# A rotary key of 32 rows: from a three-product step of its own to plain float32 products between the gates

## The chip, the cores and the metric

The kernel runs on one core of a Trainium2 chip. The metric is the device time of one execution in microseconds (us). An execution of the kernel before takes 1001.8 us, the median of 3 runs (998.82 to 1003.82).

The engines are named as the profile names them: PE is TensorE (PEld its weight loads), DVE is VectorE, ACT is ScalarE, POOL is GpSimd, SP is the engine that issues nearly all DMAs here (SPq its queue). Each engine takes its instructions in the order in which they were written, so an instruction that waits holds back all that stand behind it on that engine.

## The reference, cut to what matters

One layer of a streaming encoder over two request groups that share weights: 512 prompt tokens and 8 x 16 sample tokens, 640 tokens of 1024 channels in all. Everything is float32.

```
h = rmsnorm(x, norm_mix_g)
z = h @ w_in                    # columns: [q down 768 | kv latent 256 | rotary key 32 | GLU 1024 | gates 2048]
latent = rmsnorm(c_kv, kv_norm_g)
k_rope = rope(k_r)              # 16 + 16 columns: [x1*cos - x2*sin, x2*cos + x1*sin]
q      = rmsnorm(c_q, q_norm_g) @ w_uq, its rotary part turned by rope
o_lat  = softmax((q_lat . latent + q_rope . k_rope) * SM_SCALE, block-causal) @ latent
conv   = silu(layernorm(depthwise conv of width 31 (GLU))) @ w_conv_out
x = x + (sigmoid(g_a) * attn + sigmoid(g_c) * conv) @ w_out
x = x + relu(rmsnorm(x) @ w_ff_up)^2 @ w_ff_down
x = x + sigmoid(rmsnorm(x) @ w_ple_gate) * (p @ w_ple_proj);  y = rmsnorm(x)
```

The change concerns `k_r` alone: 32 of the 4128 columns of `w_in`, and the turning of `k_rope`, which is an output and a part of the attention's keys.

## The kernel before, in words

All activations lie transposed: channels on the 128 partitions, the 640 tokens in the columns, worked on in two halves of 320. The layer's first part is a row of *products*, each with 1024 channels in eight blocks of 128: six of the GLU (after a start of two), `kv` 0 and 1, `kr`, `cq` 0 to 5 (the query's down-projection), `qr` 0 and 1 and `qn` 0 to 3 (the query's up-projection, six blocks each), the gates `sc` 0 to 7 and `sa` 0 to 7, then `co`. After them a planner orders the attention, the feed-forward part and the rest by a table of costs; the change doesn't touch it.

A product is exact to nearly float32 by splitting both operands: a weight slab is rounded by ACT to its `hi` part (L288), DVE or POOL subtracts to get the `lo` part (L291), the input likewise, and `mms` (L333) multiplies hi by hi, hi by lo and lo by hi: 3 x 8 blocks x 2 halves = 48 matmuls of 320 columns. `fetch` (L261) loads a slab of 512 KB from SP into one of three raw buffers; it waits until the `lo` part of the slab three before has been made. `slab` (L305) keeps three slabs split ahead.

`product` (L345) also sets the order around it. First it runs the callbacks that are due in the queue "start", then it issues some conv taps (`taps`, L516: DVE's taps at L482 and L486, ACT's at L502 and L503, which POOL adds up at L511), then the pending `lo` subtractions, then its matmuls, and at last the callbacks due in the queue "after". `start(n, f)` and `after(n, f)` put a callback n products ahead. Work that needs a chain over several engines is spread in this way: `chain` (L648) takes a column sum on PE (L403), forms 1/rms per token (L641 to L645), spreads it with a diagonal (L420) and a product with ones (L396, a matmul in plain float32), and evacuates the row (L430). For `kv` it goes on to `lat_out` (L672: two multiplications on DVE, L674, and the split of the latent, L361 and L362) and `lat_new` (L683). For `cq` it gives `cbc`.

Each `cq` product is split when it ends, by ACT (L364) and DVE (L365); ACT squares the rest (L446) and POOL sums it (L447), and the `qr` products need all six splits.

The step in question, L695 to L713: `product("kr", ...)` is a product like the others but 64 columns wide (the 32 rows, and the same rows with their halves swapped), then DVE multiplies both parts by r1 (1/rms of x, L700 and L701), POOL by cos (L702), DVE by sin (L703), and a product later DVE adds (L706); the result is stored twice (L710, L711). It stands between `kv1` and `cq0`, with two conv taps of its own (`KR_TAPS`).

PSUM holds three matmul tiles of two banks in this part (`mm_ps`, L200) beside one for the conv. The SBUF slots `Q` (L193) are 10 KB per partition each; `cqA` takes three of them from `cq0` until `qn3` has ended.

## Time and profile before

| | us |
|---|---|
| median of 3 runs | 1001.8 (998.82, 1001.8, 1003.82) |
| the profiled execution | 999.03 |
| its span in the profile | 997.1 |
| PE busy | 968.3 (97%) |
| PEld busy | 933.5 (94%) |
| DVE busy | 798.5 (80%) |
| ACT busy | 507.1 (51%) |
| POOL busy | 371.4 (37%) |

The span is cut into 40 slices of 25 us on the page; the digits are tenths busy. The products up to the gates lie in the first 10 slices:

```
PE   8999999999999999999997999999999999999996
DVE  7596899995554887687789999999999999995445
PEclk9999999999999999999999999999999999999998
```

Matmuls are pipelined: a record of 305 ns stands for one whose successor starts 147 ns later, so a busy PE is read by the starts, not by the durations. A record's start in a timeline is where the engine took it up, `x2` counts merged neighbours, and the bracket at the end of a row is the engine's idle time before it and what ended it.

### The profile page before, as it was taken

The page shows a single profiled execution, that of the slowest core. Times are in us where ns is not written, and L with a number is a line of the kernel's source. Part 1 is how long each engine was busy: PE and PEld are TensorE (multiplying, and loading weights), DVE is VectorE, ACT ScalarE, POOL GpSimd, SP SyncE. Part 2 cuts the span into 40 slices and gives each one's busy share as a digit, 9 for nine tenths or more (in the row PEclk, how much of TensorE's full clock was granted, in tenths as well). Part 3 has the DMA queues.
Part 4 walks back from the last instruction along what each step waited for, and adds up shares of the span by engine and source line. Part 5 has one row for each costly group of instructions (what it writes and reads, how often), then busy time and mean ns, then how long its engine had stood idle before and what let it go on. Part 6 is the DMA issues. An engine that isn't in the chain of part 4 may idle for free.

```text
span 997.1 us, 17043 instructions
## 1 busy us (share of the span) xinstructions
PE 968.3 (97%) x6570; PEld 933.5 (94%) x6570; DVE 798.5 (80%) x1417; ACT 507.1 (51%) x941; POOL 371.4 (37%) x270
## 2 busy tenths in 40 slices
PE   8999999999999999999997999999999999999996
PEld 8999989999999667799997999999999999999995
DVE  7596899995554887687789999999999999995445
ACT  7344544223443687635665455555555555645443
POOL 0354469322201444001239435454545454323111
PEclk9999999999999999999999999999999999999998
DMA  7329313312242433414221232322222222342203
GB/s 236 115 81 91 100 48 91 125 67 85 64 132 71 135 103 117 129 47 133 95 66 62 66 90 85 98 86 86 85 86 85 85 85 85 114 125 65 85 1 106
DMA packets 34705, 92.53 MB, mean 93 GB/s; under 512 B 8800, under 2 KB 11488, under 8 KB 34624
## 3 DMA queue, kind: packets, MB, share of 16 engines
q1 hardware_dynamic: 34480, 91.42, 30.6%
q8 instruction: 52, 0.85, 0.3%
q14 instruction: 29, 0.24, 0.1%
q10 hardware_dynamic: 144, 0.03, 0.0%
HBM read 86.12 MB, written 3.91 MB: 90 GB/s over the span
## 4 chain that ended last, share of the span: by engine, by line
PE 83%; DVE 11%; DMA 2%; issue 1%; ACT 1%; POOL 1%; SPq 0%; DVEq 0%; POOLq 0%; ACTq 0%
PE a L1919 11%; PE da L2186 9%; PE sa L343 6%; PE sc L343 6%; PE wo L1688 6%; PE b L1919 5%; PE db L2186 5%; PE pg L2482 3%; DVE cv L486 3%; PE ao L1625 3%; PE co L343 3%; PE pd L2302 3%; PE c L1919 3%; PE dc L2186 2%; PE pg L2561 2%; PE qn L343 2%
## 5 line engine op out<-in xcount | busy, mean ns | idle before, releaser
L2142 POOL TENSOR_TENSOR lo_B<-raw_down,hi_B 128x768 fp32r<-128x768 f32 x28 | 51.8, 1849 | 44.1 <-PE da L2186 27.1
L486 DVE SCALAR_TENSOR_TENSOR cv<-uP,keep,cv 128x512 f32<-128x512 f32 x87 | 65.6, 754 | 2.4
L2223 DVE TENSOR_TENSOR x<-da,x 128x320 f32<-128x320 f32 x112 | 53.9, 486 | 3.1 <-PE da L2186 0.9
L511 POOL TENSOR_TENSOR acc<-acc,tap 128x640 f32<-128x640 f32 x30 | 49.1, 1636 | 10.2 <-ACT tap L503 8.8
L2186 PE MATMUL da<-f,hi_B 128*128 128x320 f32 x224 | 50.2, 310 | 0.0
L2186 PE MATMUL da<-f,hi_A 128*128 128x320 f32 x224 | 49.6, 307 | 0.0
L2186 PE MATMUL db<-f,hi_A 128*128 128x320 f32 x224 | 49.5, 307 | 0.0
L1715 POOL TENSOR_TENSOR ssum<-ssum,sq 128x640 f32<-128x640 f32 x7 | 11.0, 1572 | 90.8 <-ACT sq L1712 90.8
L2123 POOL TENSOR_TENSOR raw_down<-raw_down 128x256 f32<-128x256 f32 x28 | 21.5, 768 | 60.7 <-DVE S L2115 60.3
L2135 ACT ACTIVATE hi_B<-raw_down 128x768 fp32r<-128x768 f32 x28 | 23.7, 848 | 31.5 <-PE a L1919 13.3
L1688 PE MATMUL wo<-mgl,hi_wo 128*128 128x320 f32 x128 | 39.5, 308 | 0.0
L1688 PE MATMUL wo<-mgh,hi_wo 128*128 128x320 f32 x128 | 39.1, 305 | 0.0
L1688 PE MATMUL wo<-mgh,lo_wo 128*128 128x320 f32 x128 | 39.0, 305 | 0.0
L2186 PEld LDWEIGHTS da<-f,hi_B 128*128 128x128 f32 x224 | 36.9, 188 | 0.7 <-DVE x L2223 0.2
L2186 PEld LDWEIGHTS da<-f,hi_A 128*128 128x128 f32 x224 | 37.1, 188 | 0.0
L2186 PEld LDWEIGHTS db<-f,hi_A 128*128 128x128 f32 x224 | 37.1, 188 | 0.0
L2135 ACT ACTIVATE hi_A<-S 128x512 fp32r<-128x512 f32 (+1 forms) x56 | 26.9, 480 | 17.4 <-DVE S L2129 17.4
L2186 PE MATMUL da<-f,lo_A 128*128 128x320 f32 x112 | 34.5, 308 | 0.8 <-DVE lo_A L2142 0.7
L2186 PE MATMUL da<-f,lo_B 128*128 128x320 f32 x112 | 34.3, 306 | 0.0
L2186 PE MATMUL db<-f,lo_A 128*128 128x320 f32 x112 | 34.2, 305 | 0.0
L2055 POOL TENSOR_TENSOR f<-y,f 128x640 fp32r<-128x640 f32 x7 | 11.7, 1672 | 59.7 <-ACT f L2048 59.7
L486 DVE SCALAR_TENSOR_TENSOR cv<-uS,keep,cv 128x128 f32<-128x128 f32 x87 | 31.0, 356 | 3.2
(686 smaller groups left out, 3771.1 us busy)
## 6 DMA issues: line engine op xcount, KB each, us to landing
raw_down<-in_w_down_dram SPq DMA_DIRECT2D x32, 512.0 KB, 3.6
raw_w_gate<-in_w_gate_dram SPq DMA_DIRECT2D x16, 512.0 KB, 3.5
raw_cache_T<-in_cache_T_dram SPq DMA_DIRECT2D x8, 512.0 KB, 3.7
raw_cache_V<-in_cache_V_dram SPq DMA_DIRECT2D x8, 512.0 KB, 3.6
raw_wo<-in_w_out_dram SPq DMA_DIRECT2D x8, 512.0 KB, 3.6
raw_pg<-in_w_pg_dram SPq DMA_DIRECT2D x8, 512.0 KB, 3.5
raw_w_glu<-in_w_glu_dram SPq DMA_DIRECT2D x6, 512.0 KB, 4.7
raw_w_cq<-in_w_cq_dram SPq DMA_DIRECT2D x6, 512.0 KB, 3.9
```

What stands on the lines that cost most here:

```text
L343: nc.tensor.matmul(ps[:m, s, :HT], w_, x_[:, s * HT : (s + 1) * HT], start=st_, stop=sp)
L486: nc.vector.scalar_tensor_tensor(out=outs[i] if j == W - 1 else sums[i], in0=src, scalar=wj, in1=sums[i], op0=ALU.mult, op1=ALU.add,)
L511: nc.gpsimd.tensor_tensor(out=acc[:, 0, :], in0=acc[:, 0, :], in1=t, op=ALU.add)
L1625: nc.tensor.matmul(ps[:, :HT], w_, x_[:, halves_[s]], start=k == 0 and n == 0, stop=k == 3 and n == 2)
L1688: nc.tensor.matmul(bx[s][:, :HT], w_, x_[:, n_], start=k == 0 and j == 0, stop=k == 7 and j == 2)
L1919: nc.tensor.matmul(bx[bank][:, :HT], w_, x_, start=first and k == 0 and i == 0, stop=k == 3 and i == 2, skip_group_check=True,)
L2135: nc.scalar.activation(bx[tile][0][:, dst], src(), AF.Identity)
L2142: eng.tensor_tensor(out=l_, in0=src(), in1=h_.bitcast(F32), op=ALU.subtract)
L2186: nc.tensor.matmul(bx[bank][:, :HT], w_, x_, start=first and n == 0 and i == 0, stop=n == 1 and i == 2, skip_group_check=True,)
L2223: nc.vector.tensor_tensor(out=d, in0=bx[bank][:, :HT], in1=d, op=ALU.add)
L2302: nc.tensor.matmul(ps[:, :HT], w_, x_, start=b_ == 0 and q_ == 0, stop=b_ == 3 and q_ == 2)
L2482: nc.tensor.matmul(bx[s][:, :HT], w_, x_[:, n_], start=k == 0 and i == 0, stop=k == 7 and i == 2)
```

## The change

The slab `w_kr` leaves the row of slabs, and the product `kr` with its taps leaves its place between `kv1` and `cq0`. A function `rotary_key` is called between `qn3` and the gates:

- it loads the sign table (`snk`), the weights (256 KB) and the first half of the raw input `xT` (512 channels x 640 tokens, 1280 KB) from SP; the weights go to the slot of `cbc`, the input to the first slot of `cqA`;
- `gain` (POOL, at the start of `sc0`) multiplies the 32 weight rows by the norm's gain, and builds `fold`, four 32 x 32 identities one below the other, with swapped halves beside them;
- `quarters(0)` (after `sc0`) multiplies the four blocks of the loaded half in plain float32, without a split; block i goes to partitions 32i to 32i+31 of one PSUM tile, that is, through columns 32i to 32i+31 of the array; then it issues the load of the second half into the same slot; `quarters(1)` (after `sc1`) adds the other four blocks;
- `parts` (start of `sc2`) evacuates by ACT, and loads the cosines again; `total` (after `sc2`) adds the four parts with one product with `fold`, 64 rows wide; `turn`, `kr_sum` and `kr_out` do what L700 to L711 did, at the starts of `sc3`, `sc4` and `sc5`.

Since a product is gone between `kv1` and `cq0`, every callback that is counted in products from `kv1` now falls one named product later: the row of `kv` (L396) comes after `cq1`, where it came after `cq0`.

```diff
--- before.py
+++ after.py
@@ -52,7 +52,7 @@
 LOCK = 0.7
 SA_TAPS = 0
 EXP_AT, QB = 2, "s"
-KV_TAPS, KR_TAPS = 4, 2
+KV_TAPS = 4
 CSQ = "DVE2"
 PSCALE = "DVE2"
 NORM = ("DVE2", "DVE2", "ACT")
@@ -230,7 +230,6 @@
 
     slabs("w_glu", 8, 1024)
     slabs("w_kv", 2, 1024)
-    slabs("w_kr", 1, 512)
     slabs("w_cq", 6, 1024)
     slabs("w_q", 6, 768)
     slabs("w_gate", 16, 1024)
@@ -691,27 +690,6 @@
 
     chain(rkv_row, ssum_kv, C, "rkv", 1.0, kv_norm)
 
-
-    snk = keep[:DR, 1792:2432]
-    nc.sync.dma_start(snk, a["rope_k"])
-    ps = product("kr", blocks(slab(), range(8), 64), hT, 64, ntaps=KR_TAPS)
-    kra = tmp([P, T], "kra")
-    krb = tmp([P, T], "krb")
-    nc.vector.tensor_tensor(out=v2(kra[:DR]), in0=ps[:DR, :, :HT], in1=v2(r1[:DR]), op=ALU.mult)
-    nc.vector.tensor_tensor(out=v2(krb[:DR]), in0=ps[DR : 2 * DR, :, :HT], in1=v2(r1[DR : 2 * DR]), op=ALU.mult)
-    nc.gpsimd.tensor_tensor(out=kra[:DR], in0=kra[:DR], in1=cos[:DR, 0, :], op=ALU.mult)
-    nc.vector.tensor_tensor(out=krb[:DR], in0=krb[:DR], in1=snk, op=ALU.mult)
-
-    def kr_sum():
-        nc.vector.tensor_tensor(out=kra[:DR], in0=kra[:DR], in1=krb[:DR], op=ALU.add)
-        start(1, kr_out)
-
-    def kr_out():
-        nc.sync.dma_start(o["kr"], kra[:DR])
-        nc.sync.dma_start(KR[64:96, :], kra[:DR])
-
-    start(1, kr_sum)
-
     def rope_pair(xa, xb, n, name, out):
 
         cs, sn = cos[:n, 0, :], cos[:n, 1, :]
@@ -791,6 +769,99 @@
             nc.scalar.activation(ap[m], g_, AF.Sigmoid)
         return t, ap
 
+
+
+
+    def rotary_key():
+        snk = keep[:DR, 1792:2432]
+        nc.sync.dma_start(snk, a["rope_k"])
+        small_ = R.get([P, T], "krw")
+        raw, fold = small_[:, :512].rearrange("p (k n) -> p k n", k=8), small_[:, 512:576]
+        wk = raw[:, :, DR:]
+        nc.sync.dma_start(raw, a["w_kr"][0].rearrange("p (k n) -> p k n", k=8))
+        xk = Q.get([P, 4, T], "xk")
+        bx = {}
+
+        def load(r):
+            nc.sync.dma_start(xk, a["xT"][r * 512 : (r + 1) * 512, :].rearrange("(i p) t -> p i t", p=P))
+
+        def gain():
+            nc.gpsimd.tensor_tensor(
+                out=wk,
+                in0=raw[:, :, :DR],
+                in1=vec[:, G_MIX : G_MIX + 8, None].to_broadcast([P, 8, DR]),
+                op=ALU.mult,
+            )
+            nc.gpsimd.tensor_tensor(out=fold[:, :DR], in0=ident[:, 0:32], in1=ident[:, 32:64], op=ALU.add)
+            for i in (2, 3):
+                nc.gpsimd.tensor_tensor(
+                    out=fold[:, :DR], in0=fold[:, :DR], in1=ident[:, 32 * i : 32 * i + 32], op=ALU.add
+                )
+            nc.gpsimd.tensor_copy(fold[:, 32:48], fold[:, 16:32])
+            nc.gpsimd.tensor_copy(fold[:, 48:64], fold[:, 0:16])
+
+        def quarters(r):
+            if r == 0:
+                bx["ps"] = mm_ps("krp")
+            for s in range(2):
+                for i in range(4):
+                    k = 4 * r + i
+                    nc.tensor.matmul(
+                        bx["ps"][32 * i : 32 * i + 32, s, :HT],
+                        wk[:, k],
+                        xk[:, i, s * HT : (s + 1) * HT],
+                        start=r == 0,
+                        stop=r == 1,
+                        skip_group_check=True,
+                    )
+            if r == 0:
+                load(1)
+                after(1, lambda: quarters(1))
+            else:
+                start(1, parts)
+
+        def parts():
+            bx["p"] = tmp([P, T], "krp")
+            nc.scalar.activation(v2(bx["p"]), halves(bx["ps"]), AF.Copy)
+            Q.free(xk)
+            bx["c"] = tmp([P, T], "krc")
+            nc.sync.dma_start(bx["c"][:DR], a["rope"][:DR, 0, :])
+            after(1, total)
+
+        def total():
+            ps = bx["ps"] = mm_ps("kr")
+            for s in range(2):
+                nc.tensor.matmul(
+                    ps[: 2 * DR, s, :HT], fold, bx["p"][:, s * HT : (s + 1) * HT], start=True, stop=True
+                )
+            R.free(small_)
+            start(1, turn)
+
+        def turn():
+            ps = bx["ps"]
+            kra = bx["a"] = tmp([P, T], "kra")
+            krb = bx["b"] = tmp([P, T], "krb")
+            nc.vector.tensor_tensor(out=v2(kra[:DR]), in0=ps[:DR, :, :HT], in1=v2(r1[:DR]), op=ALU.mult)
+            nc.vector.tensor_tensor(
+                out=v2(krb[:DR]), in0=ps[DR : 2 * DR, :, :HT], in1=v2(r1[DR : 2 * DR]), op=ALU.mult
+            )
+            nc.gpsimd.tensor_tensor(out=kra[:DR], in0=kra[:DR], in1=bx["c"][:DR], op=ALU.mult)
+            nc.vector.tensor_tensor(out=krb[:DR], in0=krb[:DR], in1=snk, op=ALU.mult)
+            start(1, kr_sum)
+
+        def kr_sum():
+            nc.vector.tensor_tensor(out=bx["a"][:DR], in0=bx["a"][:DR], in1=bx["b"][:DR], op=ALU.add)
+            start(1, kr_out)
+
+        def kr_out():
+            nc.sync.dma_start(o["kr"], bx["a"][:DR])
+            nc.sync.dma_start(KR[64:96, :], bx["a"][:DR])
+
+        load(0)
+        start(1, gain)
+        after(1, lambda: quarters(0))
+
+    rotary_key()
     sc_t, sc = gate("sc", GATE_TAPS)
 
     def conv_end():
```

How the instructions stand now, engine by engine. On DVE, from the diagonal of `kv` to the taps of `cq2` (`cq_1000` is the PSUM of `cq0`, `cq_1070` that of `cq1`; `cv` are conv taps), before:

```order
L420 TENSOR_TENSOR dg_rkv<-ident,rkv 128x640
L706 TENSOR_TENSOR kra<-kra,krb 32x640
L291 TENSOR_TENSOR lo_w_cq_992<-raw_w_cq_827,hi_w_cq_991 128x1024
L365 SCALAR_TENSOR_TENSOR cq_987<-cq_1000,vec,cq_986 128x640
L674 SCALAR_TENSOR_TENSOR kv<-kv,vec,rkv 128x640 x2
L362 TENSOR_TENSOR latHL<-kv,latHL 128x1024
L291 TENSOR_TENSOR lo_w_cq_1058<-raw_w_cq_905,hi_w_cq_1057 128x1024
L365 SCALAR_TENSOR_TENSOR cq_987<-cq_1070,vec,cq_986 128x640
L486 SCALAR_TENSOR_TENSOR cv_453<-uP,keep,cv_453 128x512
```

and now (`cq_912` is the PSUM of `cq0`, `cq_983` that of `cq1`):

```order
L364 SCALAR_TENSOR_TENSOR cq_902<-cq_912,vec,cq_901 128x640
L419 TENSOR_TENSOR dg_rkv<-ident,rkv 128x640
L290 TENSOR_TENSOR lo_w_cq_976<-raw_w_cq_827,hi_w_cq_975 128x1024
L364 SCALAR_TENSOR_TENSOR cq_902<-cq_983,vec,cq_901 128x640
L673 SCALAR_TENSOR_TENSOR kv<-kv,vec,rkv 128x640 x2
L361 TENSOR_TENSOR latHL<-kv,latHL 128x1024
L485 SCALAR_TENSOR_TENSOR cv_453<-uP,keep,cv_453 128x512
```

The two multiplications of `kv` and the split of the latent stood between the splits of `cq0` and `cq1`; they now stand behind that of `cq1`, in front of the taps of `cq2`.

On SP, from the last stores of the rotary query on (`raw_w_gate_1748` and `raw_w_gate_1671` are the same slab, of `sc3`), before:

```order
L758 DMA qT_1434<-o_q 16x640 x4
L267 DMA raw_w_gate_1748<-in_w_gate_dram 128x1024
L267 DMA raw_w_gate_1809<-in_w_gate_dram 128x1024
L267 DMA raw_w_gate_1882<-in_w_gate_dram 128x1024
L267 DMA raw_w_gate_1951<-in_w_gate_dram 128x1024
```

and now:

```order
L736 DMA qT_1357<-o_q 16x640 x4
L266 DMA raw_w_gate_1671<-in_w_gate_dram 128x1024
L777 DMA keep<-in_rope_k_dram 32x640
L781 DMA krw<-in_w_kr_dram 128x512
L786 DMA xk<-in_xT_dram 128x4x640
L266 DMA raw_w_gate_1737<-in_w_gate_dram 128x1024
L786 DMA xk<-in_xT_dram 128x4x640
L266 DMA raw_w_gate_1830<-in_w_gate_dram 128x1024
L266 DMA raw_w_gate_1910<-in_w_gate_dram 128x1024
L828 DMA krc<-in_rope_dram 32x640
```

Three loads now stand behind the slab of `sc3`: of these, that of the weights waits for the last DVE read of `cbc`, and the first load of `xk` for PE's reads of `cqA` in `qn3`. The second load of `xk`, and with it all slabs behind it, waits until PE has ended `quarters(0)`.

On PE, around the end of `sc0` (`sc_1764` is `sc0`, `sc_1847` is `sc1`); before, the rows of `sc1` follow those of `sc0` at once:

```order
L343 MATMUL sc_1826<-hTh_96,hi_w_gate_1672 128x320 x2
L343 MATMUL sc_1826<-hTl_98,hi_w_gate_1672 128x320 x2
L343 MATMUL sc_1826<-hTh_96,lo_w_gate_1673 128x320 x2
L343 MATMUL sc_1896<-hTh_95,hi_w_gate_1745 128x320 x2
L343 MATMUL sc_1896<-hTl_97,hi_w_gate_1745 128x320 x2
```

and now:

```order
L342 MATMUL sc_1764<-hTl_98,hi_w_gate_1595 128x320 x2
L342 MATMUL sc_1764<-hTh_96,lo_w_gate_1596 128x320 x2
L809 MATMUL krp<-xk,krw 32x320 x8
L342 MATMUL sc_1847<-hTh_95,hi_w_gate_1668 128x320 x2
L342 MATMUL sc_1847<-hTl_97,hi_w_gate_1668 128x320 x2
```

The eight matmuls of `quarters(0)` wait for the load of `xk` and for POOL's `gain`, and `sc1` stands behind them. Eight more stand between `sc1` and `sc2`, and the two of `total` between `sc2` and `sc3`; the 48 of `kr` are gone.

## Rows read from the trace of the kernel before

**Rows 1.** Busy time by stretch; columns: stretch, length, five engines, PEclk, DMA share, GB/s.

```profile
80.81:87.86 7.05, 7.05 (x51) 6.50 (x49) 4.37 (x6) 4.32 (x8) 4.80 (x3) 1.00 1.68 38
...
126.50:133.40 6.90, 6.90 (x50) 6.90 (x49) 6.69 (x10) 4.05 (x7) 4.29 (x3) 1.00 0.22 61
...
169.70:176.73 7.03, 7.03 (x50) 7.03 (x49) 6.70 (x12) 1.97 (x3) 6.79 (x4) 1.00 0.44 126
176.73:226.00 49.27, 49.27 (x338) 49.27 (x337) 46.21 (x81) 11.81 (x14) 13.54 (x6) 1.00 0.24 84
```

**Rows 2.** Timeline of PE from kr to qn; columns: start, us, what, idle before.

```profile
80.81 0.46 PE L343 MATMUL kr<-hTh,hi_w_kr 128*64 128x320 f32 x2
...
87.86 1.17 PE L403 MATMUL ps_rkv<-ones,ssum_kv 128*128 128x1 f32 x10
...
96.81 0.51 PE L396 MATMUL psb_rkv<-dg_rkv,ones 128*128 128x320 f32 x1 [0.64 <-DVE dg_rkv L420]
...
133.38 0.45 PE L343 MATMUL qr<-cq,hi_w_q 128*128 128x320 f32 x2
...
139.25 1.28 PE L403 MATMUL ps_cbc<-ones,ssum_cq 128*128 128x1 f32 x10 [0.43 <-POOL ssum_cq L447]
...
147.42 1.32 PE L396 MATMUL psb_cbc<-dg_cbc,ones 128*128 128x320 f32 x4 [1.51 <-DVE dg_cbc L420]
```

**Rows 3.** Timeline of DVE, from the end of kr to that of qn3.

```profile
95.12 0.81 DVE L703 TENSOR_TENSOR krb<-krb,keep 32x640 f32<-32x640 f32 x1 [2.65 <-DMA keep<-in_rope_k_dram]
...
99.65 0.88 DVE L365 SCALAR_TENSOR_TENSOR cq<-cq,vec,cq 128x640 fp32r<-128x640 f32 x1 [1.11 <-ACT cq L364]
100.45 1.67 DVE L674 SCALAR_TENSOR_TENSOR kv<-kv,vec,rkv 128x640 f32<-128x640 f32 x2
103.26 1.22 DVE L362 TENSOR_TENSOR latHL<-kv,latHL 128x1024 fp32r<-128x1024 f32 x1 [1.14 <-ACT latHL L361]
...
106.52 0.89 DVE L365 SCALAR_TENSOR_TENSOR cq<-cq,vec,cq 128x640 fp32r<-128x640 f32 x1 [0.91 <-ACT cq L364]
...
113.29 0.88 DVE L365 SCALAR_TENSOR_TENSOR cq<-cq,vec,cq 128x640 fp32r<-128x640 f32 x1 [0.43 <-ACT cq L364]
...
135.88 0.87 DVE L365 SCALAR_TENSOR_TENSOR cq<-cq,vec,cq 128x640 fp32r<-128x640 f32 x1
...
171.11 1.65 DVE L772 TENSOR_TENSOR qT<-qn,cbc 64x640 f32<-64x640 f32 x2
```

**Rows 4.** Timeline of POOL: the sum of squares behind the last cq split.

```profile
137.63 1.57 POOL L447 TENSOR_TENSOR ssum_cq<-ssum_cq,sqcq 128x640 f32<-128x640 f32 x1 [2.49 <-ACT sqcq L446]
```

**Rows 5.** Chain that ended last: a product of two plain float32 matmuls, four records.

```profile
233.22 1.07 PE ps_mu L396 x4
```

**Rows 6.** Timelines of SP and PE at the gates.

```profile
161.93 11.50 SPq L758 DMA_DIRECT2D qT<-o_q  x16
173.54 3.31 SPq L267 DMA_DIRECT2D raw_w_gate<-in_w_gate_dram  x3
...
176.73 0.46 PE L343 MATMUL sc<-hTh,hi_w_gate 128*128 128x320 f32 x2
```

**Rows 7.** DMA issues; columns: KB each, median us from issue to landing.

```profile
raw_w_gate<-in_w_gate_dram SPq DMA_DIRECT2D x16, 512.0 KB, 3.5
...
kT<-in_cache_krT_dram SPq DMA_DIRECT2D x24, 64.0 KB, 1.9
...
pT<-in_pT_dram SPq DMA_DIRECT2D x1, 640.0 KB, 5.0
```

**Rows 8.** Two stretches with a full DMA queue, columns as in Rows 1.

```profile
12.00:14.00 2.00, 2.00 (x15) 2.00 (x14) 2.00 (x4) 2.00 (x4) 0.00 (x0) 1.00 1.03 411
25.00:30.00 5.00, 5.00 (x37) 4.79 (x36) 1.07 (x3) 0.00 (x0) 1.19 (x1) 1.00 0.89 348
```

**Rows 9.** Three stretches at the attention's start, columns as in Rows 1.

```profile
332.00:336.00 4.00, 2.87 (x20) 2.21 (x18) 3.57 (x14) 2.80 (x8) 0.54 (x2) 1.00 0.79 256
336.00:340.00 4.00, 3.72 (x12) 2.36 (x13) 3.85 (x9) 3.88 (x11) 1.76 (x1) 0.60 0.42 138
340.00:344.00 4.00, 4.00 (x26) 3.03 (x26) 3.89 (x14) 2.24 (x10) 2.39 (x5) 0.97 0.20 41
```

## The prediction

> **What bounds the kernel now.** I read the busy times of the page first, then PE's waits, then the stretches and the timelines of the engines around the step, then SP's queue. PE is busy 97% of the span, and in the products up to the gates it waits three times: 0.64 us at `psb_rkv`, 0.43 at `ps_cbc`, 1.51 at `psb_cbc`, and nothing else until the attention; so these stages are bound by PE's columns, and a product taken out is worth its length unless another engine is late. The reader is to see in the stretches how near that is: while `cq` 5 runs, DVE is busy 6.69 of 6.90 us, in `sc0` 6.70 of 7.03, over the next seven gates 46.21 of 49.27 [rows 1]. And the bounds are already DVE's at one place: DVE splits `cq5` at 135.88, 2.5 us after PE began `qr0` at 133.38, and ACT's square, POOL's sum (137.63 + 1.57) and `ps_cbc` at 139.25 hang on it [rows 2 to 4].
>
> **What is removed.** `kr` runs from 80.81 to 87.86 on PE, 7.05 us [rows 2]. The diagonal of `kv` is late because DVE first waits 2.65 us for the sign table that `krb` needs [rows 3]; that DMA goes elsewhere, so the 0.64 us before `psb_rkv` go too, and nothing follows in its place: the diagonal then has a whole `cq` product as cover. PE thus reaches `cq2` 7.05 + 0.64 = 7.69 us earlier. The slab's split, the two conv taps and the four DVE operations of about 0.81 us each leave this place; DVE idles there anyway (4.37 of 7.05 us busy [rows 1]).
>
> **What DVE takes back.** The callbacks now fall one `cq` later. `cq0` and `cq1` have no conv taps, `cq2` has three. Before, the latent's work (1.67 us for `kv` twice, 1.14 of waiting for ACT, 1.22 for the split) stood in front of the split of `cq1`, in a stretch where DVE had room. Now it stands behind it, in front of the taps. DVE starts that split 99.65 - 96.81 = 2.84 us after `psb_rkv` in both cases, since ACT copies the row first [rows 2, 3]. With `psb_rkv` 0.64 us earlier, at about 96.2, the split of `cq1` starts at 99.0. Before, from there to the end of the split of `cq5` it was 135.88 + 0.87 - 106.52 = 30.23 us, of which 0.43 were idle. Now it is 30.23 - 0.43 + 1.67 + 1.14 + 1.22 = 33.8, so the last split ends at 132.8 instead of 136.75: 3.9 us earlier, not 7.7. From that split to `psb_cbc` the chain is the same, so `qn` begins 3.9 us earlier, and **3.8 of the 7.7 us are given back** as waits of PE in `qr0`, which reaches its last block 4.4 us after its start, and at `ps_cbc`. From below: if DVE's subtractions run faster with POOL elsewhere, nothing is given back (0); from above, another 0.5 for as much slip in four products. I take 3.8.
>
> **What is added on PE.** 16 products of 320 columns, 32 wide, in plain float32, and two for the sum. The trace has no matmul of this width beside others. Two plain float32 products take 1.07 us, in two records each [rows 5], so 0.535 a product and 0.27 a record. One after the other the 16 take 8.6, with the sum 9.6 us. Four fully side by side they take a quarter, 2.1, with the sum 3.2. Between them: PE takes records in order, and the second record of a product goes through the same columns as the first, so it holds up the next product until the first record is through; then only the second record of one and the first of the next overlap, 8 x 0.27 + 0.27 = 2.4 a round, 4.8 for both, with the sum **5.9 us**. I take this, the middle, since no row is near either end.
>
> The Trainium skill, in "TensorEngine Tiling (Array Packing)", section "Tiling Modes", holds that tiles of 128 x 32 load and multiply independently, which would make it the 3.2; no run here shows it yet. The same section says that changing the mode drains the engine, which speaks against the change: four changes in two rounds.
>
> **The wait that is added.** `quarters(0)` stands behind `sc0`, which ends at 176.73 in the clock of before; all that follows is in this clock, since SP, DVE and PE move together from `psb_cbc` on. SP is busy with the 16 stores of the rotary query from 161.93 until 173.43, then issues the slab of `sc3` at 173.54 [rows 6]. Behind it come the sign table, the weights, which also wait for DVE's last read of `cbc` (171.11 + 1.65 = 172.76, no delay [rows 3]), and the first load of `xk`: three issues of about 0.4 us, so `xk` is issued at about 174.8, 2 us before `sc0` ends. A 64 KB load lands after 1.9 us, 512 KB after 3.5, 640 KB after 5.0 [rows 7]; `xk` has 1280 KB, 1.31 MB. Taking 1.5 us until bytes flow, the queue is at the slab's last bytes at about 176.8; then 0.26 MB of weights and 1.31 MB go at 348 GB/s, the rate of a full queue in 25 to 30 us [rows 8], in 4.5 us and land with 0.3 more at 181.7. **PE stands for 5.0 us.** From below, with no queue ahead and 411 GB/s, 174.8 + 1.5 + 3.2 = 179.5, 2.8 us; from above, at the slope from 64 to 640 KB (3.1 us for 0.59 MB, 190 GB/s), 174.8 + 1.9 + 6.6 = 183.3, and behind the weights 184: 7.3. POOL's `gain` waits for the weights, on land at about 178, and is 256 columns where the sum of 640 takes 1.57 us [rows 4]: done before `xk`. The slabs of `sc1` and `sc2` are already loaded, and `sc1` stands behind the wait.
>
> PE's clock: after a stretch in which PE was busy 2.87 of 4 us the granted clock was 0.60, then 0.97, so mostly at 1.2 GHz of the two levels for one stretch; that lost (0.40 + 0.03) x 4 = 1.7 us [rows 9]. A PE that stands 5 us does less than that, so I add **1.7**, between 0 and 3.
>
> The second load is issued when `quarters(0)` has ended, with nothing ahead: 1.5 + 1.31/0.348 + 0.3 = 5.6 us, and `sc1` covers it with 7.0. So 0, up to 1.5 at the slower slope (8.5). What stands behind on SP are the slabs of `sc4` on; each is wanted two products later, so they cost 0.
>
> **What is moved, at nothing.** DVE gets four operations of 0.81 us at `sc3` and `sc4` and the two taps, 5.5 us in all, over a stretch with 3.06 to spare and about 10 us more from PE's own delay; without that cover the rest, 2.4 us, would be late at most. One tap more stands after `sc7`; `sa0` covers it. The ring of PSUM tiles gets `krp` and `kr`; their readers run a product ahead of the reuse. The keys are wanted only after `co`. POOL's `gain` and `fold` delay the slab of `sc2`, which the same wait of PE covers.
>
> **The sum.** -7.05 - 0.64 + 3.8 + 5.9 + 5.0 + 1.7 = **+8.7 us**. Against the profiled execution's 999.03 that is 1007.7; the runs shown have their median 2.8 us above it, and the forecast is of a median: 1001.8 + 8.7 = 1010.5, so 1010.
>
> **The rivals.** *Full overlap*: 3.2 instead of 5.9, so +6.0, 1008. Against it stand the two records of each product. The Trainium skill's rule on tiles, above, would have it so. *No overlap*: 9.6, +12.4, and with `quarters(0)` at the lower clock about 2 more, 1016. For it: not one record of before shows two matmuls whose columns run together. *DVE gives nothing back and the load comes early*: -7.69 + 5.9 + 2.8 = +1.0, 1003, the same within what can be told. For it: the subtractions on DVE take 1.2 to 2.5 us with what POOL does; against it: all three bounds must fall together. *The other side, faster*: the load of `xk` is hidden. It decides at 176.73: if SP issued `xk` before about 171, since SP ends the stores of the query early, PE doesn't stand, the clock stays, and with full overlap it is -3.9 + 3.2 = -0.7, and with nothing given back -4.5, 997. Against it: the first load also waits for PE's own `qn3`, which ends at 169.7, and SP is busy until 173.43.
>
> **How the numbers follow.** Chances: half overlap as summed 0.45, no overlap 0.20, full overlap 0.20, nothing given back 0.10, hidden load 0.05. A measurement of this kernel can tell about 0.5%, 5 us, from no change. Half overlap is slower by that in 0.42 of its 0.45, no overlap always, full overlap in half of its cases, the others not: slower 0.72; the last, where the load is hidden, gives faster with a little of the fourth: 0.06; the same 0.22. The likeliest case's own range is +4 to +13, 1006 to 1015. For 8 in 10 it runs from nothing given back (1003, and 1 below for the median's own spread) to no overlap with the slower clock and the slower load (-3.9 + 9.6 + 7.3 + 3 + 1.5 = +17.5): 1002 to 1019.
>
> **What would show it.** Right: PE waits about 5 us for `xk` before the first `krp`; about 2.7 us in `qr0` for DVE's split of `cq5`, 1.5 each at `ps_cbc` and `psb_cbc`, none at `psb_rkv`; `psb_cbc` 3.9 us earlier; starts of the `krp` records about 0.27 apart with 2.4 us a round; a granted clock below 1 behind the wait. Wrong: no wait at the first `krp`, `psb_cbc` over 6 us earlier, or a round of 1.1 or 4.3 us.

## The result and the profile after

The changed kernel takes 1010.47 us, the median of 5 runs (1010.15 to 1015.73), beside 1003.38 us for the kernel before (5 runs, 998.82 to 1003.87, the three shown before the prediction among them). The ratio is 1.010, 95% interval 1.0074 to 1.0127: slower by 7 to 13 us; the two medians alone would give 1.007, since the runs of the kernel before spread over 5 us. The profiled execution took 1012.26 us (span 1010.4), where that of before took 999.03 (span 997.1).

The waits of PE between 60 and 300 us are four; [rows 2] had three, of 0.64, 0.43 and 1.51 us. Columns: total us, times, longest.

```profile
PE krp L809 <- DMA xk<-in_xT_dram: 6.3, 1, 6.3
PE ps_mu L395 <- DVE lnsum L879: 1.6, 1, 1.6
PE ps_cbc L402 <- POOL ssum_cq L446: 1.6, 1, 1.6
PE qr L342 <- DVE cq L364: 1.5, 1, 1.5
```

The timeline of PE, as in [rows 2] (start, us, what, idle before):

```profile
96.44 1.24 PE L395 MATMUL psb_rkv<-dg_rkv,ones 128*128 128x320 f32 x4
...
132.23 0.56 PE L342 MATMUL qr<-cq,hi_w_q 128*128 128x320 f32 x2 [1.49 <-DVE cq L364]
134.66 2.29 PE L402 MATMUL ps_cbc<-ones,ssum_cq 128*128 128x1 f32 x10 [1.57 <-POOL ssum_cq L446]
143.83 1.24 PE L395 MATMUL psb_cbc<-dg_cbc,ones 128*128 128x320 f32 x4
179.49 2.36 PE L809 MATMUL krp<-xk,krw 128*32 128x320 f32 x16 [6.26 <-DMA xk<-in_xT_dram]
181.78 0.90 PE L342 MATMUL sc<-hTh,hi_w_gate 128*128 128x320 f32 x2
190.40 1.28 PE L809 MATMUL krp<-xk,krw 128*32 128x320 f32 x16
```

And the chain that ended last, in the same place (start, us, what):

```profile
179.49 2.36 PE krp L809 x16
181.85 8.62 PE sc L342 x48
190.47 1.22 PE krp L809 x16
191.68 7.23 PE sc L342 x48
198.92 1.24 PE kr L834 x4
```

The first `krp` waits 6.26 us and then runs twice as long as the second (2.36 against 1.22), and the gate behind it takes 8.62 us where the next takes 7.23: the clock. In the same chain of the kernel before the eight gates take 56.32, or 7.04 each, so 0.19 of the 7.23 come with every round:

```profile
169.86 56.32 PE sc L343 x384
```

The stretches show the clock, and that DVE, too, does nothing there (columns as in [rows 1]):

```profile
136.00:140.00 4.00, 4.00 (x17) 4.00 (x18) 2.95 (x5) 1.75 (x4) 2.75 (x3) 0.50 0.05 14
...
173.00:179.50 6.50, 0.24 (x4) 0.04 (x3) 6.18 (x12) 2.59 (x4) 3.83 (x8) 0.89 0.88 304
179.50:183.50 4.00, 4.00 (x22) 2.36 (x23) 1.82 (x4) 0.00 (x0) 4.00 (x3) 0.50 0.16 27
183.50:187.50 4.00, 4.00 (x24) 4.00 (x24) 0.00 (x0) 0.00 (x0) 3.04 (x2) 0.83 0.98 378
```

How the difference builds up, from the starts of the same products in the two timelines:

| PE starts | before | after | shift | what lies between |
|---|---|---|---|---|
| `qr0` | 133.4 | 125.9 | -7.5 | the old `kr` and the wait at `psb_rkv` are gone |
| `psb_cbc` | 147.4 | 143.8 | -3.6 | waits in `qr0` and at `ps_cbc`, clock at 1.2 GHz |
| `sc1` | 176.73 | 181.78 | +5.05 | wait for `xk` 6.3, first round 2.36 |
| `sc2` | 183.8 | 191.6 | +7.8 | `sc1` 1.6 longer, second round 1.2 |
| `ps_mu` | 233.05 | 244.18 | +11.1 | `kr` sum 1.2, gates behind the small products 0.3, wait for `lnsum` 1.6 |
| `co` | 285.6 | 296.8 | +11.2 | nothing |

What comes behind `kn` (+11.3) adds 2.0 us more in this pair of executions. The change doesn't touch that part, and in the kernels of this study, which share it, the stretch from `kn` to the attention's output takes from 104.6 to 110.0 us (104.6 in the kernel before, 106.0 in the changed one). So in this profile the change itself is worth 11 us. In a second one, that of experiment 8, whose edit leaves PE's work as it is, it is 8.1 us at `co`: the wait for `xk` is 5.4 us instead of 6.3, the gate behind the first round 7.53 instead of 8.62, and `ps_cbc` runs at the full clock. Both lie inside the interval of the ratio, and 3 us at `co` between two single profiles are no effect by themselves.

Two more rows matter later. The rotation's product with the sine took 0.81 us in the kernel before [rows 3]; now it is

```profile
201.87 3.80 DVE L849 TENSOR_TENSOR krb<-krb,keep 32x640 f32<-32x640 f32 x1
```

while POOL works beside it:

```profile
201.07 1.56 POOL L848 TENSOR_TENSOR kra<-kra,krc 32x640 f32<-32x640 f32 x1 [5.48 <-DVE kra L844]
202.60 2.39 POOL L290 TENSOR_TENSOR lo_w_gate<-raw_w_gate,hi_w_gate 128x1024 fp32r<-128x1024 f32 x1
```

### The profile page after: what moved, and what is told of

Read it like the earlier page. It is cut to its first block, busy times and chain, and to the rows that moved or that the text cites. A ratio compares the mean times of both kernels' runs of the same rounds, so it can differ in the third digit from the quotient of the medians.

```text
span 1010.4 us, 17034 instructions
## 1 busy us (share of the span) xinstructions
PE 972.5 (96%) x6558; PEld 934.9 (93%) x6558; DVE 799.8 (79%) x1416; ACT 506.6 (50%) x941; POOL 372.8 (37%) x276
## 4 chain that ended last, share of the span: by engine, by line
PE 79%; DVE 12%; issue 3%; DMA 2%; ACT 2%; POOL 1%; SPq 1%; DVEq 0%; POOLq 0%; ACTq 0%
PE a L1990 10%; PE da L2257 9%; PE wo L1759 5%; PE b L1990 5%; PE sa L342 5%; PE db L2257 4%; DVE cv L485 4%; PE pg L2553 3%; PE ao L1696 3%; PE co L342 3%; PE pd L2373 3%; PE c L1990 3%; PE glu_b L342 2%; PE glu_a L342 2%; PE dc L2257 2%
## 5 line engine op out<-in xcount | busy, mean ns | idle before, releaser
L769 ACT ACTIVATE sc<-scr 128x640 f32<-128x640 f32 x8 | 5.9, 739 | 59.1 <-DVE scr L768 59.1
```

## The experiments

Twelve kernels beside the changed one. The ratio is to the kernel before, run with each set. The sets (1 to 4, 5 to 8, 9 to 11, 12) ran on four chips, so kernels of different sets are compared by their ratios and not by their medians.

| kernel | median us | ratio (95%) |
|---|---|---|
| the changed kernel | 1010.47 | 1.0100 (1.0074 to 1.0127) |
| 1 late round | 1006.84 | 1.0045 (1.0027 to 1.0062) |
| 2 taps forward | 1007.65 | 1.0057 (1.0037 to 1.0077) |
| 3 both | 1001.40 | 0.9989 (0.9972 to 1.0007) |
| 4 one group, on 1 | 1012.66 | 1.0095 (1.0067 to 1.0123) |
| 5 pairs by group, on 3 | 1001.06 | 0.9988 (0.9970 to 1.0006) |
| 6 loads on ACT | 1006.52 | 1.0040 (1.0023 to 1.0058) |
| 7 sine in another form, on 3 | 1000.62 | 0.9972 (0.9959 to 0.9986) |
| 8 that alone | 1012.17 | 1.0093 (1.0064 to 1.0122) |
| 9 sine on POOL, on 3 | 998.62 | 0.9961 (0.9945 to 0.9977) |
| 10 three more taps at `cq0`, on 3 | 998.37 | 0.9962 (0.9943 to 0.9980) |
| 11 = 9 and 10 | 996.97 | 0.9946 (0.9926 to 0.9966) |
| 12 sine from PSUM, on 3 | 997.58 | 0.9961 (0.9942 to 0.9979) |

**The wait for `xk`, from two sides.** Experiment 1 moves TensorE's first round behind the next gate:

```diff
-        after(1, lambda: quarters(0))
+        after(2, lambda: quarters(0))
```

> The first quarters are queued behind two gate products in place of one, so they run after sc1; nothing else is changed. Theory (TensorE stands for the load of xk, and its clock falls for it): sc1 follows sc0 at 173, ends near 180.1, and xk, which landed at 179.3, is there: the wait of 6.3 us goes, krp's first round takes 1.2 instead of 2.36 us, sc1 7.0 instead of 8.6, and ps_mu's wait for lnsum shrinks from 1.6 to under 1. About 10 us less than the changed kernel: near 1000. The second load is issued at about 181.3, lands near 187 and has until 188. Rival (the wait only stands in for one behind DVE): ps_mu or a later product waits by as much more, time stays at 1008 to 1011.

The wait is gone and the round is short, as the timeline of PE shows (columns as above):

```profile
180.65 1.28 PE L809 MATMUL krp<-xk,krw 128*32 128x320 f32 x16
...
236.43 1.60 PE L395 MATMUL ps_mu<-lnsum,ones 128*128 128x320 f32 x4 [2.20 <-DVE lnsum L879]
```

`sa0` starts at 227.0 instead of 235.4, 8.4 us earlier. But `ps_mu` then waits longer, not shorter, 2.20 us, and the clock falls behind it:

```profile
237.00:241.00 4.00, 4.00 (x16) 3.68 (x15) 3.35 (x5) 2.94 (x5) 0.00 (x0) 0.57 0.39 131
```

so 6.2 us are left at `co`, and the time is 1006.84, not near 1000. The theory of the wait holds; my reading of `ps_mu` (DVE late because it had stood idle with PE) was wrong: the rival was right about a part. DVE is late by itself.

Experiment 6 leaves PE's order as the change has it and brings the load forward: `xk` and `krw` are issued by ACT, which isn't held up by the stores of the query.

```diff
-        nc.sync.dma_start(raw, a["w_kr"][0].rearrange("p (k n) -> p k n", k=8))
...
-            nc.sync.dma_start(xk, a["xT"][r * 512 : (r + 1) * 512, :].rearrange("(i p) t -> p i t", p=P))
+            (nc.sync if r else nc.scalar).dma_start(xk, a["xT"][r * 512 : (r + 1) * 512, :].rearrange("(i p) t -> p i t", p=P))
...
         load(0)
+        nc.scalar.dma_start(raw, a["w_kr"][0].rearrange("p (k n) -> p k n", k=8))
```

> The changed kernel, with the order of TensorE's work as it is; only the first load of xk and that of krw are issued by ScalarE, where they stand behind the last query product's taps and not behind SP's sixteen pieces of the query rows, xk first. Theory (PE stands because the load is issued at 170.9 and lands 8.3 us later): xk is issued as soon as the query rows are read, near 166, lands at 173 to 175, krw near 175; the wait of krp falls from 6.3 to 0 to 2 us, its first round and sc1 run at full clock, and PE is 5 to 8 us earlier at sc2; at ps_mu 5 to 8 less what DVE keeps (2), so 1004 to 1007, as with the late round. Rival (the load lands when the weight slabs ahead of it are through, wherever it is issued): landing stays near 179 and the time near 1010.

The tile `xk` in its trace, and the waiting round:

```profile
L785 ACTq DMA_DIRECT2D xk<-in_xT_dram x1: 393/393/393, 164.1 to 164.1; - x1
```

```profile
174.00 1.28 PE L808 MATMUL krp<-xk,krw 128*32 128x320 f32 x16 [1.17 <-POOL krw L788]
```

`xk` is issued at 164.1 instead of 170.94, the wait is 1.17 us and is now for the weights; PE is 7.9 us earlier at `ps_mu`, and `ps_mu`'s wait of 1.6 stays. Late product or early load: by the ratios the same 0.5 to 0.6% against the changed kernel. The rival, a landing time set by the slabs ahead, is out.

**What DVE gives back before `psb_cbc`.** Experiment 2 has as many conv taps, other places:

```diff
-CQ_TAPS, QN_TAPS, GATE_TAPS = (0, 0, 3, 4, 4, 4), (0, 1, 2, 4), 5
+CQ_TAPS, QN_TAPS, GATE_TAPS = (0, 3, 3, 3, 3, 3), (0, 1, 2, 4), 5
```

> Conv taps per query product 0,3,3,3,3,3 instead of 0,0,3,4,4,4 (the same 15 in all), rotary key as in the changed kernel. Theory (about 4 of the 7.5 us that PE comes earlier to qr0 are given back because DVE is behind with cq5's split and the statistic): three taps, 3.5 us, go into DVE's 4.07 us idle behind cq0; cq5's split comes some 2 to 3.5 us earlier, the waits of qr0 (1.5) and ps_cbc (1.6) go or fall under 0.5 each, the clock stays at 1, and psb_cbc starts at 140 to 141.5 instead of 143.8. sc0 comes as much earlier, the wait for xk stays near 6. Time 2 to 4 us under the changed kernel: near 1007. Rival (the three taps push the split of cq1 or the norm of the key rows, so that a later product waits): psb_cbc within 0.5 us of 143.8 and the time as in the changed kernel.

```profile
131.29 1.17 PE L402 MATMUL ps_cbc<-ones,ssum_cq 128*128 128x1 f32 x10
138.63 1.31 PE L395 MATMUL psb_cbc<-dg_cbc,ones 128*128 128x320 f32 x4 [0.79 <-DVE dg_cbc L419]
173.66 2.36 PE L809 MATMUL krp<-xk,krw 128*32 128x320 f32 x16 [5.56 <-POOL acc L510]
```

Both waits are gone and `psb_cbc` starts 5.2 us earlier, more than expected, since the clock no longer falls behind the waits. The room was there in the changed kernel: in front of the split of `cq1` DVE stood 4.07 us.

```profile
99.20 0.88 DVE L364 SCALAR_TENSOR_TENSOR cq<-cq,vec,cq 128x640 fp32r<-128x640 f32 x1 [4.07 <-ACT cq L363]
```

The wait for `xk` stays (the bracket names a POOL operation of the conv; but `xk` was issued at 165.4 and landed 8.0 us later, at 173.4, 0.26 us before the round, as 0.24 in the changed kernel, and POOL's `gain` had ended at 170.9). Experiment 3 has both edits.

> Both edits of the two kernels before. If the two losses are separate, the gains add: some 10 and some 3 us under the changed kernel, near 997, about 5 us faster than the kernel before. If the second is only hidden by the first (PE comes earlier and DVE is late again at ps_mu), ps_mu waits 2 to 4 us and the time is that of the late round alone, near 1000.

They add up: `sa0` is 13.9 us earlier than in the changed kernel (8.4 and 5.6 for the single edits), and the time is that of the kernel before. The extra gain over it isn't there: `ps_mu` waits 2.12 us, the clock falls behind it, and the two gates that follow take 1.6 us longer than in experiment 9, which has no such wait.

**How the eight products overlap.** Experiment 4, on the late round, sends all blocks through the same 32 columns of the array; PSUM then does the sum, and the last product reads 32 partitions.

```diff
-                        bx["ps"][32 * i : 32 * i + 32, s, :HT],
+                        bx["ps"][:32, s, :HT],
...
-                        start=r == 0,
-                        stop=r == 1,
+                        start=k == 0,
+                        stop=k == 7,
```

> On the kernel with the late first round: all eight blocks go through the one group of columns 0 to 31 and add up in PSUM, and the product that adds the blocks takes 32 partitions instead of 128. Theory (a round of 8 products in four groups takes 1.2 us because the four overlap fully): without overlap each product of 320 columns takes about 0.53 us as in kr's sum (1.24 for 2, 1.07 for 2 in ps_mu), a round 4.3 to 5, so 6 to 7 us over two rounds on top of the late round: near 1007. Rival (the products are short because they use 32 columns only, whatever group): rounds stay at 1.2 to 1.3 us and the time stays at that of the late round.

```profile
179.13 4.49 PE L809 MATMUL krp<-xk,krw 128*32 128x320 f32 x16
190.77 4.49 PE L809 MATMUL krp<-xk,krw 128*32 128x320 f32 x16
```

4.49 us a round, 0.56 a product, like the 0.535 of [rows 5]; four groups take 1.28 by the same view. The overlap is full, and it is the groups that give it, not the 32 columns; without it the kernel takes 5.8 us more (1012.66 against 1006.84). Experiment 5, on both edits, changes the order of the eight.

```diff
-            for s in range(2):
-                for i in range(4):
+            for i in range(4):
+                for s in range(2):
```

> On the kernel with the late round and the taps moved: the eight products of a round are issued group by group (both halves of the columns in group 0, then both in group 1, ...) instead of 0,1,2,3,0,1,2,3. Theory A (products overlap with a neighbour only when it has another group, as many as stand next to each other): of 8 products 3 pairs of neighbours still differ, a round takes 2.2 to 2.6 us instead of 1.2, two rounds add 2 to 3 us: 1003.5 to 1004.5. Theory B (each group has a queue of its own): a round stays at 1.2 to 1.3 us and the time at 1001.4.

```profile
174.99 1.30 PE L809 MATMUL krp<-xk,krw 128*32 128x320 f32 x16
```

The order doesn't matter: two products of one group in a row do not hold up the next group. Theory B.

**Why DVE is late at `lnsum`.** The last suspect was the sine's 3.80 us. Experiments 7 (on both edits) and 8 (alone) write it in the form that the conv taps have, which stay at 0.76 us beside POOL:

```diff
-            nc.vector.tensor_tensor(out=krb[:DR], in0=krb[:DR], in1=snk, op=ALU.mult)
+            nc.vector.scalar_tensor_tensor(
+                out=krb[:DR], in0=krb[:DR], scalar=1.0, in1=snk, op0=ALU.mult, op1=ALU.mult
+            )
```

> On the kernel with the late round and the taps moved: DVE multiplies krb by the sine with scalar_tensor_tensor in place of tensor_tensor. Theory (the 3.80 us of that product on DVE, against 0.81 in the kernel before, are a wait for POOL's two operations beside it; the conv taps, which are scalar_tensor_tensor, keep their 0.76 beside POOL): it takes 0.8 to 0.9 us, DVE comes 2.9 us earlier to lnsum, ps_mu's wait of 2.1 us goes, and the clock's fall behind it (some 1.6 us): 3 to 4 us under that kernel, 997.5 to 998.5, 4 us faster than the kernel before. Rival (the 3.8 us are the operation's own on its operands): it stays over 3 us, and so does the time, 1001.4.

> The changed kernel with that one edit of the sine's product alone. Theory: DVE is 2.9 us earlier at lnsum, ps_mu's wait of 1.6 us goes and nothing else moves: 1.5 to 2 us under the changed kernel (about 1008.5). The waits for xk (6.3), in qr0 (1.5) and at ps_cbc (1.6) stay as they are. Rival (lnsum's wait comes from DVE's 9.2 us idle behind the gate's product and not from the sine): ps_mu waits as long as before this edit and the time stays at 1010.

The theory's edit failed in both. The tile `krb` in the first of them (duration min/median/max in ns, first and last start):

```profile
L849 DVE SCALAR_TENSOR_TENSOR krb<-krb,keep x1: 3782/3782/3782, 194.7 to 194.7; 32x640 f32<-32x640 f32 x1
```

So it isn't the form, and `ps_mu` waits 2.1 and 1.6 us as without the edit. That leaves 7 a repeat of 3 and 8 a repeat of the changed kernel: 0.2 and 0.1% apart by their ratios, inside the intervals. (Single profiles differ more: `co` starts at 283.1 in 7 and at 285.0 in 3.) What the view does show is when it ends: DVE at 198.52, POOL's second operation beside it (start 195.46, 2.38) at 197.84, 0.68 before. The kernel before has the same in its subtractions, whose inputs both lie in SBUF: 1.21 us with POOL idle, 2.54 beside POOL, which ends 1.1 us before the second of them does.

```profile
97.33 1.21 DVE L291 TENSOR_TENSOR lo_w_cq<-raw_w_cq,hi_w_cq 128x1024 fp32r<-128x1024 f32 x1
...
118.67 2.54 DVE L291 TENSOR_TENSOR lo_w_cq<-raw_w_cq,hi_w_cq 128x1024 fp32r<-128x1024 f32 x1
```

```profile
116.90 3.22 POOL L511 TENSOR_TENSOR acc<-acc,tap 128x640 f32<-128x640 f32 x2 [0.33 <-ACT tap L503]
```

Experiment 9 gives the sine to POOL, behind the cosine.

```diff
-            nc.vector.tensor_tensor(out=krb[:DR], in0=krb[:DR], in1=snk, op=ALU.mult)
+            nc.gpsimd.tensor_tensor(out=krb[:DR], in0=krb[:DR], in1=snk, op=ALU.mult)
```

> On the kernel with the late round and the taps moved: krb's product with the sine is done by POOL, behind kra's with the cosine, in place of DVE. Theory (on DVE it stood 3.8 us because it ended only 0.7 us behind POOL's two operations beside it): on POOL it takes 1.55 us like kra's, DVE goes on to its taps 3.8 us earlier, and lnsum's end comes 3 to 4 us earlier, so ps_mu no longer waits 2.1 us; sc4's weights low part on POOL comes 1.55 us later, and is waited for by nothing. 2 to 3.5 us under that kernel: 998 to 999.5. Rival (the operands are slow, or DVE is held up again by POOL at its next operation): POOL's takes over 3 us, or lnsum comes at the same time, and the time stays at 1001.

```profile
L849 POOL TENSOR_TENSOR krb<-krb,keep x1: 1560/1560/1560, 195.9 to 195.9; 32x640 f32<-32x640 f32 x1
```

1.56 us, and `lnsum`'s second sum starts at 226.17 instead of 229.89 (the first row is of experiment 3, the second of 9):

```profile
229.89 0.82 DVE L879 TENSOR_TENSOR lnsum<-lnsum,lnsum 128x640 f32<-128x640 f32 x1
226.17 0.82 DVE L879 TENSOR_TENSOR lnsum<-lnsum,lnsum 128x640 f32<-128x640 f32 x1
```

`ps_mu` doesn't wait, the clock stays: 3.8 us at `co`, of which 2.1 are the wait and 1.6 the clock. The operands are not slow. Experiment 12 keeps operation, engine and place, and changes only where one input lies, PSUM instead of SBUF:

```diff
-                out=v2(krb[:DR]), in0=ps[DR : 2 * DR, :, :HT], in1=v2(r1[DR : 2 * DR]), op=ALU.mult
+                out=ps[DR : 2 * DR, :, :HT], in0=ps[DR : 2 * DR, :, :HT], in1=v2(r1[DR : 2 * DR]), op=ALU.mult
...
-            nc.vector.tensor_tensor(out=krb[:DR], in0=krb[:DR], in1=snk, op=ALU.mult)
+            nc.vector.tensor_tensor(out=v2(krb[:DR]), in0=ps[DR : 2 * DR, :, :HT], in1=v2(snk), op=ALU.mult)
```

> On the kernel with the late round and the taps moved: DVE leaves kr times r1 in its PSUM tile and multiplies from there by the sine into krb, so that each of the two operations has one input in SBUF; operation, engine and place stay. Theory (DVE stood 3.8 us because both inputs of the sine's product lay in SBUF while POOL worked on SBUF; the conv taps beside it, whose running sum lies in PSUM, keep 0.76 us): it takes 0.8 to 0.9 us beside POOL's two operations of 1.55 and 2.39, lnsum comes 3 us earlier, ps_mu doesn't wait: 998 to 999.5, as with the sine on POOL. Rival (POOL's use of any kind holds DVE there, or 32 partitions from another place are slow): it stays over 3 us, ps_mu waits 2.1 us and the time is 1001. The Trainium skill's page SBUF — State Buffer, section Who interferes with whom, has it that a DVE instruction with two SBUF inputs contends with a GpSimd one that reads SBUF and one with a single SBUF input does not; by that it is the first.

```profile
L849 DVE TENSOR_TENSOR krb<-kr,keep x1: 816/816/816, 194.7 to 194.7; 32x640 f32<-32x640 f32 x1
```

with POOL beside it as before:

```profile
193.90 1.56 POOL L848 TENSOR_TENSOR kra<-kra,krc 32x640 f32<-32x640 f32 x1 [5.47 <-DVE kra L844]
195.42 2.39 POOL L290 TENSOR_TENSOR lo_w_gate<-raw_w_gate,hi_w_gate 128x1024 fp32r<-128x1024 f32 x1
```

0.82 us instead of 3.78, 4.3 us at `co`, 997.58 us. This shows the cause: with both inputs in SBUF the operation stood here until both of POOL's, which read SBUF, were through; with one in PSUM it didn't. It also gives the reason why 7 and 8 failed: the form was not what spares the conv taps; like the sine's product of 12 they have one input in PSUM, their running sum. The Trainium skill, "SBUF — State Buffer", section "Who interferes with whom", says the same (a DVE instruction with two SBUF inputs contends with a GpSimd one that reads SBUF); this pair of runs agrees with it, 3.78 against 0.82.

Experiment 10 leaves the sine alone and brings the conv forward in front of `cq0`, and 11 has both.

```diff
-CQ_TAPS, QN_TAPS, GATE_TAPS = (0, 3, 3, 3, 3, 3), (0, 1, 2, 4), 5
+CQ_TAPS, QN_TAPS, GATE_TAPS = (3, 3, 3, 3, 3, 3), (0, 1, 2, 4), 5
```

> On the kernel with the late round and the taps moved: three more conv taps in front of cq0's product (3,3,3,3,3,3), sine on DVE as it was. Theory (DVE's 3.8 us idle in front of ps_rkv takes three taps of 1.18, and everything that hangs on DVE's conv comes 3.5 us earlier): the last tap and lnsum come 3.5 us earlier, ps_mu no longer waits; psb_rkv and psb_cbc start within 0.5 us of where they did: 998 to 999.5. Rival (the taps stand ahead of the low part of cq1's weights, or of the statistic rkv, which PE needs): cq1 or psb_rkv waits 1 to 3 us and the gain is lost: 1001 to 1002.

> Both edits of the two kernels before. One of them is enough to take ps_mu's wait of 2.1 us away, so the second brings nothing: the time is that of the better of the two within 1 us (998 to 999.5), 0.3 to 0.5 per cent under the kernel before. If each only takes part of the wait, this one alone loses it all, and is 1 to 2 us under both.

In 10 the second sum for `lnsum` starts at 226.69 (229.89 in 3) although the sine takes its 3.79 us:

```profile
195.29 3.79 DVE L849 TENSOR_TENSOR krb<-krb,keep 32x640 f32<-32x640 f32 x1
...
226.69 0.82 DVE L879 TENSOR_TENSOR lnsum<-lnsum,lnsum 128x640 f32<-128x640 f32 x1
```

`ps_mu` doesn't wait, and neither do `cq1` and `psb_rkv` (0.4 us of waiting shows up at the first `krp`). So what bound was DVE's total, and either saving covers it. 11 is within the intervals of 9, 10 and 12, as it should be if one is enough, and has the lowest median: **996.97 us, 0.3 to 0.7% under the kernel before and by the ratios some 1.5% under the changed one.** 9, 10 and 12 can't be told from it.

## Why the prediction was right, and where its steps were not

The forecast, 1010 us and slower, came out at 1010.47. The direction and its two main causes, the wait for `xk` and what DVE takes back, were right; that the number agrees to half a microsecond is luck, since several terms were off and with both signs. The case that came true for the products, full overlap, stands in the prediction with 1008. Step by step, in the prediction's order:

- *Removed*, -7.69 forecast: `qr0` comes 7.5 us earlier and `psb_rkv` doesn't wait. Right.
- *What DVE takes back*, 3.8: 7.5 - 3.6 = 3.9. Right in size and cause (experiment 2 gives it back), not in place. Forecast were 2.7 in `qr0` and 1.5 each at `ps_cbc` and `psb_cbc`; it was 1.5, 1.6 and none, because the clock, which I hadn't counted here, fell to 0.50 from 136 to 140 and the slower `qr1` gave DVE the time (in experiment 2, at the full clock, `psb_cbc` waits 0.79).
- *The products*, 5.9: **this term failed.** The step was "the second record of a product goes through the same columns as the first, so it holds up the next product"; the 16 records of a round take 1.22 us at the full clock, so the second records don't hold up the next product. With the sum that is 1.2 + 1.2 + 1.24 = 3.7, and with 0.19 more in each of the three gates behind them 4.2 (in experiment 9 the eight gates with these products take 60.55 us, without them 56.32 in the kernel before). That is the rival of full overlap, to which I gave 0.20; experiments 4 and 5 show that it is the four groups that give it, in any order. The first round's 2.36 us agree with the forecast sign of 2.4 by accident: they are the same 1.2 at half the clock.
- *The wait*, 5.0 of 2.8 to 7.3: 6.26. `xk` was issued at 170.94, where the forecast, 174.8 in the clock of before less the 3.7 of the shift, has 171.1. Too small was the landing: 8.3 us against 6.9. The stretch of the wait moved 304 GB/s, not 348. The same load alone took 5.7, as forecast (5.6), and was hidden.
- *The clock*, 1.7 of 0 to 3: 1.1 in the first round and 1.4 in `sc1` (8.62 against 7.23), 2.5.
- *At nothing*: **this failed too.** I priced the moved DVE operations at 0.81 us, their length in the kernel before, where POOL did nothing beside the sine (its last operation there, the row below, had ended at 93.3, and the sine starts at 95.12 [rows 3]), and took PE's delay for DVE's cover. The sign was in the prediction itself, which says that DVE's subtractions take 1.2 to 2.5 us with what POOL does, and wasn't applied to the operations that move. The sine took 3.8 us beside POOL, and the delay was no cover: DVE takes its work in order and stood 9.18 us for `sc1`'s product. The first row is of the kernel before, the second of the changed one.

```profile
91.70 1.56 POOL L702 TENSOR_TENSOR kra<-kra,keep 32x640 f32<-32x640 f32 x1 [1.00 <-DVE kra L700]
```

```profile
190.58 0.82 DVE L768 TENSOR_TENSOR scr<-sc,r 128x640 f32<-128x640 f32 x1 [9.18 <-PE sc L342]
```

The bill is `ps_mu`'s 1.6 us.

So the forecast of +8.7 stands against +11.1 in the profiles: the wait 1.3 more, the clock 0.8, `lnsum` 1.6, what is given back and removed 0.3, the products 1.7 less; 0.1 is left. Errors of both signs made the total nearer than its terms.

The rival on the other side, the hidden load with -0.7 to -4.5, was rightly judged as a case that this kernel isn't, but its price was short of a condition. Hidden in experiments 1 and 6, the load still left the kernel 0.4% slower; only with DVE's two delays gone as well is the kernel faster, 4.4 us at `co` in experiment 9 (281.2 against 285.6). Of these 7.69 - 4.2 = 3.5 are the smaller product (with the old wait at `psb_rkv`). The rest, about 1 us, is that the kernel before waits 0.43 and 1.51 us at `ps_cbc` and `psb_cbc` and experiment 9 only 0.8 at the second. In that the moved taps have a part, and no run moves them in the kernel before, so what they alone are worth there is not shown.

Open: the time of the landing behind other loads was only seen, not taken apart; and why the clock fell behind `ps_mu`'s wait of 2.1 us in experiment 3 and not behind the same wait in 7. It isn't the kernel alone that decides: the changed kernel and 8, the same up to there, run the ten records of `ps_cbc` in 2.29 and 1.27 us behind the same waits.

## What to carry to other kernels

A product that is made smaller and moved is worth its columns only if the engine that feeds the next wait has room there: look up which engine ends that wait, and give it the same microseconds back (here three conv taps in another place were worth 5.4 us, 1006.84 against 1001.40 with the late round, and the smaller product saves PE 3.5). Price a DVE operation by where its inputs lie and what POOL does at the new place, not by its length at the old one. And time an engine stands for a neighbour that stands is not cover for more work on it, since it takes its instructions in order.

## What the runs showed of the hardware

- Eight plain float32 products of 320 columns, 32 wide, in four groups of columns take 1.22 us, in any order; in one group 4.49. Two products 128 wide take 1.07 [rows 5], and the gate behind a round takes 7.23 instead of 7.04, so all that can be put down to going over to the narrow groups and back is about 0.34 us a round. The Trainium skill, "TensorEngine Tiling (Array Packing)", section "Tiling Modes", says that tiles work independently, which these runs bear out, and that a change of the mode drains the engine, which costs no more than this here.
- A DVE product of 32 x 640 with both inputs in SBUF took 3.78 to 3.80 us beside POOL's operations of 1.55 and 2.39, in either form, and 0.82 with one input in PSUM.
- A wait of PE can cost the clock again: 1.5 and 1.6 us in `qr0` and at `ps_cbc` were followed by 4 us at 0.50, 2.2 us at `ps_mu` by 4 us at 0.57. But in experiment 7 a wait of 2.1 us at the same place left it at 1.00 (columns as in [rows 1]):

```profile
230.00:234.00 4.00, 3.47 (x20) 3.18 (x21) 3.63 (x5) 2.12 (x3) 0.00 (x0) 1.00 0.35 105
234.00:238.00 4.00, 4.00 (x30) 4.00 (x29) 4.00 (x4) 2.67 (x5) 2.43 (x2) 1.00 0.07 27
```
